# GpSimd taken out of the SSD mixer's groups: masks to ScalarE, products and sums to VectorE

## The chip, the cores and the metric

The kernel runs on one core of a Trainium2 chip. A core has five engines that run at the same time, each with its own instruction stream in a fixed order: TensorE (PE in the profile, PEld for its weight loads), VectorE (DVE), ScalarE (ACT), GpSimd (POOL), and SyncE (SP), which here issues DMA transfers. Instructions of different engines wait for each other through semaphores. The metric is the device time of one execution in microseconds (us).

## What is computed

Two transformer-like blocks of two layers each, on 256 latent tokens and 256 context tokens of width 1024. The first block's second layer holds the SSD mixer (a state space scan with 8 groups of 4 heads), which is where the change lies:

```python
def ssd_chunk_scan(xs, dt, a, bm, cm, s0):
    ...
    def step(s, inp):
        xi, dti, bi, ci = inp
        cum = jnp.cumsum(dti * a, axis=1)
        seg = cum[:, :, None] - cum[:, None, :]
        decay = jnp.exp(jnp.where(mask, seg, -jnp.inf))
        xdt = xi * dti[..., None]
        cb = jnp.einsum('bign,bjgn->bijg', ci, bi)
        y = jnp.einsum('bijg,bijgr,bjgrp->bigrp', cb, decay, xdt)
        y = y + jnp.einsum('bign,bigr,bgrpn->bigrp', ci, jnp.exp(cum), s)
        ...
def ssd_mixer(uc, ul, w_in, conv_w, conv_b, dt_bias, a_log, d_skip, norm_g, w_out, need_ctx):
    ...
        z, xbc, dt = jnp.split(h @ w_in, [SSD_DI, SSD_DI + SSD_CONV_DIM], axis=-1)
        xbc = jax.nn.silu(dwconv(xbc, conv_w, conv_b))
        ...
        y = (y_f + y_b[:, ::-1] + xs * d_gr).reshape(b, l, SSD_DI)
        return rms_norm(y * jax.nn.silu(z), norm_g) @ w_out, (s_f, s_b)
```

`y_f` and `y_b` are the scans forwards and backwards; both start from the states that the context tokens leave.

## The kernel before

All matrix products with weights go through `gemm`. It streams a weight in units of 128x1024 float32 (tile `wr`, three buffers), and `_unit` splits each into a high part `wh` (line 395, a cast on ScalarE) and a low part `wl` (line 400, a subtraction on the engine that `loeng` names at that time). There are two buffers each of `wh` and `wl`. The matmuls of line 439 then take high times high and low (`wh` with `xh` and `xl`), and low times high (`wl` with `xh`). So per unit the cast, then the subtraction, have to be done before TensorE comes to the unit.

The mixer's function `ssd` goes over 8 groups `g`. A group has four units of convolution channels (24 matmuls each, mostly of 512 columns), and two units for the gate `z` (24 matmuls of 256 columns each), whose `wl` is made on the engine that `SLO` names. The convolution is lines 1200 to 1210 (tiles `scv`, `sth`, `sxc`), then come transposes (L1244), scaled copies `sxs` and `sxk` (L1189) and the states (L1265, L1273). After that, for each of two token tiles `t`, this is done (shortened):

```python
                for d in range(2):
                    for i, x in enumerate((dah.bitcast(F32), dal)):
                        rt = self.t([P, 4, P], "srt", NRT, F32R)
                        ...
                        if RTE[i] == "s":
                            for r in range(4):
                                nc.scalar.mul(out=rt[:, r, :], in_=tri_in[:, d, :], mul=x[:, t, c + r:c + r + 1])
                        else:
                            eng = nc.vector if RTE[i] == "v" else nc.gpsimd
                            eng.tensor_tensor(out=rt, in0=tri_in[:, d, None, :].to_broadcast([P, 4, P]),
                                              in1=bc(x[:, t, c:c + 4], P), op=ALU.mult)
                        nc.tensor.matmul(out=p, lhsT=strict[:, d, :], rhs=rt.rearrange("p r c -> p (r c)"),
                                         start=d == 0 and i == 0, stop=d == 1 and i == 1)
```

These masks `srt` (two high, from `sdh`, and two low, from `sdl`; three buffers) feed four matmuls (L1302). Their exponential is `sL` (L1305). `sM` is made on ScalarE (L1310) and VectorE (L1315), then multiplied by `sL` (L1317, on the engine that `ME` names). L1327 multiplies it with the values. `syi` holds the part that comes from the state (L1322); two sums (L1331 and L1332, on GpSimd where `YP` is 1) and L1333 and L1334 finish the tile as `syg`, and L1340 transposes it.

The code is written group after group, but a scheduler sets the order of the instructions on each engine when the program is built, by its own estimates of how long each takes. So TensorE's stream has the next groups' weight products woven between one group's mixer steps, and other background work (`aps`, L533) too.

Of the kernel before, what the change touches and what calls it, by code (L numbers as in the profile page):

```python
# [29 lines left out]
EPRIO = 500  # L30
FSTOP = 7
SBEG = 0
SLO = "gpsimd"
MPOOL = (1,)
NRT = 3
RTE = "sg"
GPRIO = 300
GF = 150
GFIN = 26
# [21 lines left out]
BRAW = 1  # L61
NBSQ = 2
NBB = 2
VE, ME = "s", "g"
ENORM = ("vector", "vector")
NBTG, NBP, NQK, NBPT = 7, 3, 8, 2
SHQ, XB2 = 1, 18
XDA, XKA, XSA, RTA, YP = 0, 0, 0, 2, 1
GRATE = (0, 0.6, 0.6, 0.6)
GAINENG = "gpsimd"  # L70
CPRIO = 4000
# [199 lines left out]
class K:  # L271
# [889 lines left out]
    def ssd(self, u, mode):  # L1161
# [29 lines left out]
        for g in range(8):  # L1191
# [39 lines left out]
            def sink_z(p, t, sz=sz):  # L1231
                th = self.t([P, 2, 256], "sth", 2)
                nc.scalar.activation(out=th[:, 0], in_=p, func=AF.Tanh, scale=0.5)
                nc.vector.scalar_tensor_tensor(out=sz[:, t, :], in0=th[:, 0], scalar=1.0, in1=p, op0=ALU.add, op1=ALU.mult)
            jobs = [("T", 0, 256, 256 + t * P, P, (lambda p, t=t: sink_z(p, t))) for t in range(2)]
            with self.lo_on(SLO, True):
                off = self.gemm(A["swin"], off, KD, 256, u, jobs)
# [44 lines left out]
            for t in range(2):  # L1282
# [8 lines left out]
# [3 lines that stand above are left out]
                        c = d * 32 + g * 4  # L1294
# [6 lines that stand above are left out]
# [1011 lines left out]
```

## Time and profile before

| what | us |
|---|---|
| median of 3 runs (lowest to highest) | 2522.02 (2516.8 to 2524.46) |
| the profiled execution, and its span from first to last instruction | 2523.41, 2521.6 |
| busy in the span: TensorE | 2392.2 (95%) |
| VectorE | 1741.5 (69%) |
| ScalarE | 1208.9 (48%) |
| GpSimd | 363.6 (14%) |

The mixer's groups lie from about 880 to 1217 us of the span. A share of busy time is an average over stages with different limits. An engine's idle time costs something only where another engine waits for it in the end, so what counts for a stage is which engine has no idle time there, and whom it waits for when it has. The span of a matmul overlaps that of the next one, so the pace of TensorE is read from the distance between starts.

### The profile page before, as it was taken

The page shows a single profiled execution, that of the slowest core. Times are in us where ns is not written, and L with a number is a line of the kernel's source. Part 1 is how long each engine was busy: PE and PEld are TensorE (multiplying, and loading weights), DVE is VectorE, ACT ScalarE, POOL GpSimd, SP SyncE. Part 2 cuts the span into 40 slices and gives each one's busy share as a digit, 9 for nine tenths or more (in the row PEclk, how much of TensorE's full clock was granted, in tenths as well). Part 3 has the DMA queues.
Part 4 walks back from the last instruction along what each step waited for, and adds up shares of the span by engine and source line. Part 5 has one row for each costly group of instructions (what it writes and reads, how often), then busy time and mean ns, then how long its engine had stood idle before and what let it go on. Part 6 is the DMA issues. An engine that isn't in the chain of part 4 may idle for free.

```text
span 2521.6 us, 36806 instructions
## 1 busy us (share of the span) xinstructions
PE 2392.2 (95%) x13879; PEld 1913.8 (76%) x13879; DVE 1741.5 (69%) x3303; ACT 1208.9 (48%) x2367; POOL 363.6 (14%) x308
## 2 busy tenths in 40 slices
PE   7999997999998899999899989999999998999997
PEld 4777776777776777787698868788777877877776
DVE  3455578866688867687755676987564566798666
ACT  3445444432323455566565455554444344564553
POOL 0011114000000124443400120100021001100010
PEclk8999998999999899999999999999999999999999
DMA  6222244555555444523465552222122353333343
GB/s 253 100 85 76 86 166 151 192 200 213 201 198 177 158 159 143 175 84 113 162 216 184 191 164 90 77 72 84 59 84 76 106 191 118 125 107 100 109 147 130
DMA packets 105394, 348.01 MB, mean 138 GB/s; under 512 B 14200, under 2 KB 20288, under 8 KB 105216
## 3 DMA queue, kind: packets, MB, share of 16 engines
q1 hardware_dynamic: 100304, 333.22, 38.6%
q0 software_dynamic: 3616, 12.06, 1.4%
q8 instruction: 109, 1.79, 0.3%
q14 instruction: 69, 0.57, 0.1%
q10 hardware_dynamic: 1296, 0.38, 0.1%
HBM read 338.75 MB, written 6.85 MB: 137 GB/s over the span
## 4 chain that ended last, share of the span: by engine, by line
PE 45%; DVE 5%; ACT 1%; issue 1%; DMA 0%; DVEq 0%; ACTq 0%
PE acc L439 37%; PE ps L1728 2%; PE ps L1756 2%; PE aps L1867 1%; PE ps L1640 1%; DVE wl L400 1%; PE aps L1772 1%; PE acc L1640 0%; DVE xl L751 0%; PE ps L741 0%; DVE by L761 0%; DMA row<-rowd 0%; ACT wh L395 0%; DVE bnm L1739 0%; DVE bP L1853 0%
## 5 line engine op out<-in xcount | busy, mean ns | idle before, releaser
L395 ACT CAST wh<-wr 128x1024 fp32r<-128x1024 f32 (+3 forms) x461 | 471.9, 1026 | 637.1 <-PE acc L439 557.4
L439 PE MATMUL acc<-wh,xh 128*128 128x512 f32 (+3 forms) x1876 | 725.2, 393 | 11.9 <-ACT wh L395 6.5
L400 DVE TENSOR_TENSOR wl<-wr,wh 128x1024 fp32r<-128x1024 f32 (+3 forms) x421 | 517.3, 1230 | 314.2 <-ACT wh L395 238.7
L439 PE MATMUL acc<-wh,xl 128*128 128x512 f32 (+3 forms) x1876 | 718.6, 388 | 7.3 <-DVE xl L1570 7.0
L439 PE MATMUL acc<-wl,xh 128*128 128x512 f32 (+3 forms) x1876 | 507.1, 386 | 5.9 <-POOL wl L400 4.0
L439 PEld LDWEIGHTS acc<-wh,xh 128*128 128x128 f32 x1876 | 356.4, 191 | 96.0 <-ACT wh L395 12.2
L439 PEld LDWEIGHTS acc<-wh,xl 128*128 128x128 f32 x1876 | 356.9, 191 | 81.2 <-DVE xl L1570 8.3
L439 PEld LDWEIGHTS acc<-wl,xh 128*128 128x128 f32 x1876 | 342.8, 189 | 84.4 <-POOL wl L400 6.2
L439 PE MATMUL acc<-xl,wh 128*128 128x512 f32 (+2 forms) x1024 | 341.1, 349 | 9.6 <-DVE xl L751 9.5
L439 PE MATMUL acc<-xh,wh 128*128 128x512 f32 (+2 forms) x1024 | 345.6, 354 | 4.2 <-ACT wh L395 2.2
L439 PE MATMUL acc<-xh,wl 128*128 128x512 f32 (+1 forms) x1024 | 231.8, 347 | 4.3 <-DVE wl L400 4.3
L439 PEld LDWEIGHTS acc<-xh,wh 128*128 128x128 f32 (+1 forms) x1024 | 197.1, 194 | 39.0 <-issue 6.3
L439 PEld LDWEIGHTS acc<-xl,wh 128*128 128x128 f32 (+1 forms) x1024 | 197.8, 194 | 35.2 <-DVE xl L751 10.7
L400 POOL TENSOR_TENSOR wl<-wr,wh 128x1024 fp32r<-128x1024 f32 x40 | 98.3, 2461 | 724.5 <-ACT wh L395 583.5
L439 PEld LDWEIGHTS acc<-xh,wl 128*128 128x128 f32 x1024 | 166.5, 191 | 37.8 <-DVE wl L400 7.1
L573 DVE SCALAR_TENSOR_TENSOR adav<-wrd,s,adav 128x512 f32<-128x512 f32 x196 | 144.5, 769 | 55.4 <-DMA wrd<-in_ada 54.2
L1742 ACT ACTIVATE bP<-ps,bnm 128x512 f32<-128x512 f32 (+1 forms) x144 | 88.5, 621 | 86.2 <-DVE bnm L1739 70.8
L1988 POOL TENSOR_SCALAR bP<-bP,brc 128x512 f32<-128x512 f32 (+1 forms) x24 | 33.4, 1396 | 489.7 <-DVE brc L1985 461.2
L1739 DVE TENSOR_REDUCE bnm<-ps 128x1 f32<-128x512 f32 (+1 forms) x120 | 78.1, 683 | 32.3 <-PE ps L1728 32.0
L1204 DVE SCALAR_TENSOR_TENSOR scv<-acc,scw,scv 128x510 f32<-128x510 f32 (+3 forms) x140 | 83.4, 633 | 14.4 <-ACT scv L1200 14.2
L1756 PE MATMUL ps<-ident,bP 128*128 128x128 f32 x400 | 60.8, 278 | 2.4 <-ACT bPT L1631 1.4
L1631 ACT COPY bPT<-ps 128x512 f32<-128x512 f32 x75 | 43.8, 595 | 33.9 <-PE ps L1756 27.9
(429 smaller groups left out, 3097.8 us busy)
## 6 DMA issues: line engine op xcount, KB each, us to landing
wr<-in_w SPq DMA_DIRECT2D x136, 512.0 KB, 3.5
wr<-in_win SPq DMA_DIRECT2D x136, 512.0 KB, 3.5
wrd<-in_ada SPq DMA_DIRECT2D x128, 512.0 KB, 4.4
wr<-in_swin SPq DMA_DIRECT2D x52, 512.0 KB, 3.5
wr<-in_gwin SPq DMA_DIRECT2D x24, 512.0 KB, 3.4
wr<-in_wbr SPq DMA_DIRECT2D x24, 512.0 KB, 3.4
wr<-in_wout SPq DMA_DIRECT2D x24, 512.0 KB, 3.5
wst<-in_ada SPq DMA_DIRECT2D x16, 512.0 KB, 7.6
```

The costliest lines, as they stand in the source:

```text
L395: nc.scalar.copy(out=hi[:, :n], in_=raw[:, :n])
L400: getattr(nc, eng).tensor_tensor(out=lo[:, :n], in0=raw[:, :n], in1=hi[:, :n].bitcast(F32), op=ALU.subtract)
L439: mm = nc.tensor.matmul(out=o, lhsT=wv if kind == "F" else xv, rhs=xv if kind == "F" else wv, start=b["first"], stop=bool(fin and b["left" ...
L573: o = nc.vector.scalar_tensor_tensor(out=a, in0=xi, scalar=c, in1=a, op0=ALU.mult, op1=ALU.add)
L1204: nc.vector.scalar_tensor_tensor(out=c[:, :, o0:o1], in0=pv[:, :, i0:i1], scalar=w[:, tap:tap + 1], in1=c[:, :, o0:o1], op0=ALU.mult, op1= ...
L1631: return self.nc.scalar.copy(out=out, in_=in_)
L1640: nc.tensor.transpose(p[:width, t * P:(t + 1) * P], x[:, j * width:(j + 1) * width], self.ident)
L1728: mms.append(self.nc.tensor.matmul(out=p[:, n * nk:(n + 1) * nk], lhsT=q[a][rows, i * P:(i + 1) * P], rhs=k[b][rows, :nk], start=m == 0, s ...
L1739: nc.vector.tensor_reduce(out=nm[:, :n], in_=p.rearrange("p (n k) -> p n k", n=n), axis=AX.X, op=ALU.max, negate=True)
L1742: nc.scalar.activation(out=e[:, i * nk:(i + 1) * nk], in_=p[:, i * nk:(i + 1) * nk], func=AF.Exp, bias=nm[:, i:i + 1], accum_out=sm[i])
L1756: mms.append(nc.tensor.transpose(p[:, d:d + P], e[:, c:c + P], self.ident))
L1988: nc.gpsimd.tensor_scalar(out=b, in0=b, scalar1=rc[:, 1, i:i + 1], scalar2=None, op0=ALU.mult)
```

## The change

Four numbers change. No other line does.

```diff
-SLO = "gpsimd"
+SLO = "vector"
...
-RTE = "sg"
+RTE = "ss"
...
-VE, ME = "s", "g"
+VE, ME = "s", "v"
...
-XDA, XKA, XSA, RTA, YP = 0, 0, 0, 2, 1
+XDA, XKA, XSA, RTA, YP = 0, 0, 0, 2, 0
```

For each group: the two low parts of the gate's weights (L400) go from GpSimd to VectorE; the four low masks (one instruction of 128x512 each at line 1300) become 16 instructions of 128x128 on ScalarE (line 1297); the two products of line 1317 and the four sums of lines 1331 and 1332 go from GpSimd to VectorE. GpSimd keeps its work outside of the groups.

The scheduler also sets a new order. Besides the mixer's groups on all engines, it differs in one later piece, in the last attention layers of the second block (TensorE's rows 9933 to 10110 of 11001, at about 2260 to 2320 us), and SyncE issues ten of the loads of the mixer's weights at other places among its own.

On ScalarE, while the second group's token tiles are done: from the cast of the third group's first gate unit (the first `wh`) to that of its second (the other `wh`); `sdh` marks high masks, `sdl` low ones, and a row with x4 is one mask. Before:

```order
L395 CAST wh_8691<-wr_8689 128x1024
L1268 COPY sS_8385<-ps_8380 128x512
L1310 ACTIVATE sM_8420<-scb_8397,sdt_7611 128x128 x4
L1200 ACTIVATE scv_8647<-acc_8507,scw_7369 128x512
L1200 ACTIVATE scv_8657<-acc_8508,scw_7369 128x512
L1297 ACTIVATE srt_8451<-tri,sdh_7641 128x128 x4
L395 CAST wh_8737<-wr_8735 128x1024
L1305 ACTIVATE sL_8418<-ps_8399 128x512
```

Now:

```order
L395 CAST wh_8715<-wr_8713 128x1024
L1305 ACTIVATE sL_8436<-ps_8411 128x512
L1297 ACTIVATE srt_8481<-tri,sdh_7641 128x128 x4
L1200 ACTIVATE scv_8671<-acc_8531,scw_7369 128x512
L1200 ACTIVATE scv_8681<-acc_8532,scw_7369 128x512
L1297 ACTIVATE srt_8487<-tri,sdl_7642 128x128 x4
L1297 ACTIVATE srt_8859<-tri,sdh_7641 128x128 x4
L1297 ACTIVATE srt_8865<-tri,sdl_7642 128x128 x4
L1310 ACTIVATE sM_8495<-scb_8466,sdt_7611 128x128 x4
L395 CAST wh_8761<-wr_8759 128x1024
```

Between the two casts stood one mask; now there are four, of which the last two already belong to the third group's first token tile, and the products `sM` of the second token tile stand right ahead of the second cast.

On VectorE at the same place: from the third group's convolution taps (L1204) on its first two channel blocks, whose results lie in banks of `acc`, to the last step `sxc` of the convolution. Before:

```order
L1204 SCALAR_TENSOR_TENSOR scv_8647<-acc_8507,scw_7369,scv_8647 128x2x255
L1204 SCALAR_TENSOR_TENSOR scv_8657<-acc_8508,scw_7369,scv_8657 128x2x255
L1322 TENSOR_TENSOR syi_8433<-ps_8430,sex_7630 128x512
L1204 SCALAR_TENSOR_TENSOR scv_8647<-acc_8507,scw_7369,scv_8647 128x2x255
L1204 SCALAR_TENSOR_TENSOR scv_8657<-acc_8508,scw_7369,scv_8657 128x2x255
L1204 SCALAR_TENSOR_TENSOR scv_8647<-acc_8507,scw_7369,scv_8647 128x2x254
L1204 SCALAR_TENSOR_TENSOR scv_8657<-acc_8508,scw_7369,scv_8657 128x2x254
L1210 SCALAR_TENSOR_TENSOR sxc_8655<-sth_8653,scv_8647 128x512
L1210 SCALAR_TENSOR_TENSOR sxc_8665<-sth_8663,scv_8657 128x512
L1204 SCALAR_TENSOR_TENSOR scv_8667<-acc_8509,scw_7369,scv_8667 128x2x254
L1204 SCALAR_TENSOR_TENSOR scv_8677<-acc_8510,scw_7369,scv_8677 128x254
```

Now:

```order
L1334 TENSOR_TENSOR syg_8406<-syi_8451,ssz_8280 128x256
L1204 SCALAR_TENSOR_TENSOR scv_8671<-acc_8531,scw_7369,scv_8671 128x2x254
L1204 SCALAR_TENSOR_TENSOR scv_8681<-acc_8532,scw_7369,scv_8681 128x2x254
L1322 TENSOR_TENSOR syi_8508<-ps_8505,sex_7630 128x512
L1315 SCALAR_TENSOR_TENSOR sM_8495<-scb_8466,sdt_7611,sM_8495 128x128 x4
L1331 TENSOR_TENSOR syi_8508<-syi_8508 128x256
L400 TENSOR_TENSOR wl_8762<-wr_8759,wh_8761 128x1024
L1332 TENSOR_TENSOR syi_8508<-syi_8508,sxk_8390 128x256
L1317 TENSOR_TENSOR sM_8495<-sM_8495,sL_8493 128x512
L1210 SCALAR_TENSOR_TENSOR sxc_8679<-sth_8677,scv_8671 128x512
L1210 SCALAR_TENSOR_TENSOR sxc_8689<-sth_8687,scv_8681 128x512
L400 TENSOR_TENSOR wl_8985<-wr_8982,wh_8984 128x1024
```

The low part of the second gate unit (the first `wl`), both sums (L1331, L1332) and the product (L1317) have come between the taps and `sxc`; that low part stands behind the four `sM` instructions and one sum.

## Rows read from the trace of the kernel before

**Rows 1.** Windows: us, then busy us (instructions) PE, PEld, DVE, ACT, POOL; clock, DMA share, GB/s.

```profile
880.00:1200.00 320.00, 307.99 (x1760) 252.26 (x1760) 239.04 (x448) 186.30 (x432) 130.29 (x98) 0.99 0.39 134
2260.00:2320.00 60.00, 59.70 (x326) 47.70 (x325) 47.87 (x120) 31.01 (x56) 0.00 (x0) 1.00 0.33 105
```

**Rows 2.** Waits of PE, 880 to 1217 us: total us, times, longest us; nine lines.

```profile
PE ps L1265 <- DVE sxs L1189: 2.9, 2, 1.5
...
PE ps L1327 <- POOL sM L1317: 1.2, 1, 1.2
...
PE acc L439 <- ACT xh L473: 0.6, 1, 0.6
```

**Rows 3.** POOL's groups, 870 to 1225 us: busy us, mean ns; idle before, releaser.

```profile
L400 POOL TENSOR_TENSOR wl<-wr,wh 128x1024 fp32r<-128x1024 f32 x17 | 40.4, 2381 | 83.8 <-PE acc L439 51.2 <-ACT wh L395 24.6 <-issue 8.0
...
L1300 POOL TENSOR_TENSOR srt<-tri,sdl 128x512 fp32r<-128x512 f32 x32 | 39.2, 1245 | 77.0 <-PE ps L1302 66.1 <-DVE sdl L1224 10.9
...
L1317 POOL TENSOR_TENSOR sM<-sM,sL 128x512 f32<-128x512 f32 x16 | 24.7, 1541 | 25.7 <-ACT sL L1305 12.5 <-DVE sM L1315 7.1 <-ACT srt L1297 4.1
...
L1332 POOL TENSOR_TENSOR syi<-syi,sxk 128x256 f32<-128x256 f32 x16 | 15.9, 996 | 0.9
...
L1331 POOL TENSOR_TENSOR syi<-syi 128x256 f32<-128x256 f32 x16 | 13.3, 831 | 20.4 <-DVE syi L1322 20.4
```

**Rows 4.** Three of DVE's groups in the same stretch, all of two operands in SBUF.

```profile
L400 DVE TENSOR_TENSOR wl<-wr,wh 128x1024 fp32r<-128x1024 f32 x44 | 59.4, 1354 | 22.2 <-ACT wh L395 21.6 <-PE acc L439 0.4
...
L1210 DVE SCALAR_TENSOR_TENSOR sxc<-sth,scv 128x512 f32<-128x512 f32 x21 | 21.2, 1014 | 0.6 <-ACT sth L1207 0.5
...
L1334 DVE TENSOR_TENSOR syg<-syi,ssz 128x256 f32<-128x256 f32 x16 | 11.5, 716 | 0.2
```

**Rows 5.** Timeline of DVE, 1069 to 1078 us: start us, us.

```profile
1074.39 2.44 DVE L1210 SCALAR_TENSOR_TENSOR sxc<-sth,scv 128x512 f32<-128x512 f32 x1
```

**Rows 6.** Timeline of POOL, the same stretch.

```profile
1073.87 2.41 POOL L400 TENSOR_TENSOR wl<-wr,wh 128x1024 fp32r<-128x1024 f32 x1
```

**Rows 7.** Three lines of code on DVE, whole span: ns least/median/most, first and last start.

```profile
L1210 DVE SCALAR_TENSOR_TENSOR sxc<-sth,scv x35: 407/679/2442, 856.3 to 1163.7; 128x512 f32<-128x512 f32 x21, 128x256 f32<-128x256 f32 x14
...
L1334 DVE TENSOR_TENSOR syg<-syi,ssz x16: 407/426/1523, 916.1 to 1212.6; 128x256 f32<-128x256 f32 x16
...
L400 DVE TENSOR_TENSOR wl<-wr,wh x421: 548/1225/3383, 36.4 to 2511.0; 128x1024 fp32r<-128x1024 f32 x131, 128x384 fp32r<-128x384 f32 x4, 128x768 fp32r<-128x768 f32 x3, 128x576 fp32r<-128x576 f32 x2
```

**Rows 8.** ACT's group of the high masks, 870 to 1225 us.

```profile
L1297 ACT ACTIVATE srt<-tri,sdh 128x128 fp32r<-128x128 f32 x128 | 41.0, 391 | 16.9 <-PE ps L1302 15.0 <-DVE sdh L1223 1.9
```

**Rows 9.** Timeline of PE, 948 to 958 us, with a wait at a gate unit.

```profile
949.66 0.39 PE L439 MATMUL acc<-xl,wh 128*128 128x512 f32 x1
949.89 0.40 PE L439 MATMUL acc<-xh,wh 128*128 128x512 f32 x1
...
950.48 0.59 PE L1320 MATMUL ps<-sS,sxc 128*128 128x256 f32 x2
950.91 0.59 PE L1320 MATMUL ps<-sT,sxc 128*128 128x256 f32 x2
...
951.46 0.28 PE L439 MATMUL acc<-xh,wh 128*128 128x256 f32 x1
951.58 0.28 PE L439 MATMUL acc<-xl,wh 128*128 128x256 f32 x1
...
954.72 0.36 PE L439 MATMUL acc<-wh,xh 128*128 128x256 f32 x1 [1.92 <-ACT srt L1297]
```

**Rows 10.** Timeline of ACT, the same stretch: the cast that PE waited for.

```profile
951.94 1.05 ACT L395 CAST wh<-wr 128x1024 fp32r<-128x1024 f32 x1 [0.87 <-ACT srt L1297]
```

**Rows 11.** Timeline of DVE, the same stretch: taps in turn on two banks.

```profile
952.52 2.71 DVE L1204 SCALAR_TENSOR_TENSOR scv<-acc,scw,scv 128x510 f32<-128x510 f32 x4
```

**Rows 12.** Timeline of PE, 962 to 967 us: a background product.

```profile
962.35 1.06 PE L533 MATMUL aps<-wrd,s 128*32 128x512 f32 x8
```

**Rows 13.** Timeline of DVE, 962 to 967 us: four instructions of line 1315.

```profile
965.43 1.13 DVE L1315 SCALAR_TENSOR_TENSOR sM<-scb,sdt,sM 128x128 f32<-128x128 f32 x4
```

## Prediction

> **What bounds the kernel now.** Begin with the windows view of the mixer's stretch [rows 1]. Between 880 and 1200 us TensorE is busy for 308.0 of 320 us, VectorE for 239.0 (75%), ScalarE for 186.3 (58%) and GpSimd for 130.3 (41%), and TensorE's granted clock is 0.99. So TensorE bounds the stage, and it can win at most its idle time: 12.0 us, 0.5% of the whole. Next look at whom it waits for in these 12 us: nine lines of the view of waits, from 2.9 down to 0.6 us [rows 2]. GpSimd ends only one of them, 1.2 us, where the product `sM` (L1317) is late for L1327. GpSimd's groups [rows 3] show why it ends so little: its masks sat for 66.1 us waiting for TensorE to free a buffer, and its low parts for 51.2 us waiting for TensorE to finish with an earlier unit. It is mostly ahead of its consumer.
>
> So the change is not read from shares. It is read from whether ScalarE and VectorE, whose streams now hold that work as well, are still ahead of TensorE at the places where TensorE takes it.
>
> **What is removed.** GpSimd loses 39.2 us of masks, 24.7 of products, 13.3 and 15.9 of sums, and 16 of its 17 low parts at 2.38 us, 38.1 [rows 3]: 131.2 us. None of that is itself on the path, except the 1.2 us.
>
> **What VectorE gets.** 16 low parts at 1.225 us are 19.6. For the 16 products of 128x512, an operation that the trace has only on GpSimd, the nearest row is another one of VectorE with two operands in SBUF and 512 columns: median 0.679, so 10.9 us. For the 32 sums of 128x256 it is L1334, median 0.426, so 13.6 [rows 7]. Together 44.1 us. The other end for a product is GpSimd's own 1.54 [rows 3], which would make it 57.8; I take the first, since it is the same engine and the same size.
>
> **What VectorE gets back.** The same three lines take longer on average in this stage than their medians [rows 4, 7]: `wl` 1.354 against 1.225, 44 times, 5.7 us; `sxc` 1.014 against 0.679, 21 times, 7.0; L1334 0.716 against 0.426, 16 times, 4.6. That is 17.3 us. A pair of rows shows where it goes: a `sxc` that begins 0.5 us after a low part on GpSimd takes 2.44 us [rows 5, 6]. That is 1.76 more than its median, and nearly the rest of GpSimd's instruction (1073.87 + 2.41 = 1076.28). Without GpSimd this falls away. VectorE's load is then 239.0 + 44.1 - 17.3 = 265.8 of 320 us, 83%.
>
> The page "SBUF — State Buffer" of the Trainium skill, section "Who interferes with whom", says why: a VectorE instruction with two inputs in SBUF and a GpSimd instruction that reads SBUF want the same port, and the one that comes second is blocked until the first is through. Rows 5 and 6 agree. By that rule everything that VectorE does late in this stage could be GpSimd's doing, which is the second rival below; by the rows it is 17.3 us of busy time, which is a gain only where TensorE was waiting.
>
> **What ScalarE gets.** 32 low masks of four instructions. The high ones are 128 instructions in 41.0 us [rows 8], so 0.32 each and 1.28 a mask; the low ones cost another 41.0. Load: 186.3 + 41.0 = 227.3 of 320 us, 71%. The path from a free buffer to a mask gets longer: GpSimd's mask took 1.25 [rows 3] beside ScalarE's, and now they come one behind the other.
>
> A rule of the skill speaks against this part: "ScalarE: Activation LUTs", section "Rules for kernel authors", sends plain products to VectorE and budgets about 0.3 us for each instruction and 0.83 ns for each element. By that a mask of four would be an estimated 1.62 us and the sum 10.9 us more ScalarE time. The rows, at 0.32 an instruction in a run of four, are what I use.
>
> **Is the work still in time?** I follow one place by hand, that of the order shown above. Count from the start of the second tile's first L1302, which frees a mask buffer. TensorE's way to the second gate unit: two more L1302 and 0.23 to the start of the next, at 0.235 each, 0.70; background products 1.06 [rows 12]; five products of the convolution, two of 512 and three of 256 columns, 0.82; L1320 0.86; the fourth L1302 0.235; the first gate unit, 24 at 0.118, 2.83. Sum 6.5 us (the distances between starts are 0.235, 0.43 for a pair of L1320, and 0.118 [rows 9]). ScalarE's way to that unit's cast: some 0.5 us until the buffer is free (an estimate: about one matmul's 0.4 us [rows 9] and a little), three masks 3.84, four `sM` taken at the same 1.28, the cast 1.05 [rows 10]: 6.7. So the high part is late by 0.2. The low part: VectorE has `sM` from ScalarE at 5.6, needs 1.13 for its own four [rows 13], 0.4 for one sum and 1.225: about 8.4, and TensorE wants it 8 matmuls (0.94) after 6.5, at 7.4. Late by 1.0, of which the high part's delay is a share. In four of the eight groups three masks, or nearly so, stand ahead of a gate unit's cast; in the later groups they stand behind it. The four are not all as tight, so I count 0.9 in each: **+3.6 us**.
>
> The other place is the accumulator. A gate unit needs a bank of `acc`, and the taps of the first channel block have to let go of it. At 954.72 TensorE stood for 1.92 us ahead of a gate unit [rows 9]. The row names ScalarE's mask, but the cast had been done at 952.99 [rows 10]; the taps on VectorE, in turn on two banks, ended between 954.5 and 955.2 [rows 11], so I take the bank to be what was missing. In the new order a low part and a product (1.225 + 0.679 = 1.9) have come between the first and the last tap of that block in two groups; in the others there is a sum, or nothing new. I count half of it in two groups: **+1.9 us**.
>
> GpSimd's own wait goes: **-1.2 us**. The other 9 us or so that VectorE and ScalarE end I leave as they are: VectorE has 27 us more in its queue and no surprises in it.
>
> The moved loads of SyncE cost nothing as long as the 16 DMA engines are at 0.39 [rows 1]. The new order at 2260 to 2320 us can win no more than TensorE's 0.3 us of idle time there; VectorE is at 80% and GpSimd idle, so I count nothing.
>
> **Sum:** 3.6 + 1.9 - 1.2 = +4.3 us on the profiled execution's 2523.41: 2527.7. That execution lies 1.4 us above the median of the runs, 2522.02, so the forecast is **2526 us**. A difference under 0.3%, 7.6 us, can't be told from none; the forecast is no measurable change, slightly on the slow side.
>
> **Rivals.**
> *ScalarE becomes the engine that TensorE waits for.* The low and high masks are made one behind the other, so each of the 16 token tiles can be late by one mask, 1.28 us: 20.5 us, 2542. For it: at the one place followed by hand ScalarE is late already; its queue holds masks of the next group ahead of a cast. Against it: 71% load, buffers filled ahead, and only half of the groups in that order. It decides once the lateness at a tile exceeds about 0.5 us in all eight groups. Chance 0.25.
> *The release of VectorE wins.* All waits that VectorE and GpSimd end go, some 10 of the 12 us; 2522 - 10 = 2512. For it: the lock of rows 5 and 6, and work that is half as long on VectorE. Against it: VectorE has more to do on balance, and half of its waits are of a kind (taps, `sxs`) that no GpSimd instruction stands in front of. Chance 0.16.
> *VectorE's burst between groups.* The two low parts (2.45 us) fall into the taps, `sxc` and `sxs` of seven group changes, where PE waits for `sxs` most [rows 2]: 7 x 2.45 = 17, 2539. Chance 0.09.
>
> **Chances and range.** Forecast 0.50, its own range 2517 to 2532. The first and third rivals are slower by over 0.3%, and so is a tail of the forecast (2529.6 lies within its range): 0.36. Faster by over 0.3%, below 2514.5: most of the second rival, 0.14. No measurable change: 0.50. The range for 8 in 10 goes from 2513, short of the whole release, to 2541, about the price of the mask on every tile.
>
> **What would show it.** Right, if TensorE's busy time over the mixer's 320 us stays within some 5 us of 308, GpSimd has next to nothing there, `sxc` and L1334 come at 0.68 and 0.43, the added ScalarE group is 41 us and the low parts of the gate 1.23 each. The waits of TensorE should name casts and low parts at gate units. Wrong, if waits for masks (`srt`) or casts add up to over 10 us, if the clock in the stage falls below 0.97, or if waits for `sxs`, `xl` and taps have gone. A difference that arises after 1240 us would speak against all of it.

## The result, and the profile after

The changed kernel takes 2541.27 us (median of 4 runs, 2536.89 to 2545.65), the kernel before 2520.51 (4 runs): a ratio of 1.0088, 95% interval 1.0069 to 1.0107. It is slower by about 21 us, where no measurable change was forecast.

All of it arises in the mixer's groups. The first product with the masks (L1302) starts at 900.0 us before and 901.4 after, the last at 1207.1 and 1230.4: the stage has grown by 21.9 us. The span has grown by 19.7 (2521.6 to 2541.3). So nothing is added behind the groups.

The windows view of the changed kernel, with the columns of [rows 1]: the mixer's 320 us, then single slices of 10 us.

```profile
880.00:1200.00 320.00, 295.39 (x1655) 241.71 (x1648) 241.04 (x477) 204.75 (x520) 12.08 (x8) 0.96 0.37 124
...
1000.00:1010.00 10.00, 7.70 (x31) 5.70 (x32) 6.34 (x18) 3.61 (x12) 0.00 (x0) 0.60 0.31 112
...
1140.00:1150.00 10.00, 6.03 (x19) 4.50 (x18) 9.05 (x21) 6.89 (x22) 0.00 (x0) 0.76 0.24 83
1150.00:1160.00 10.00, 10.00 (x54) 8.61 (x53) 3.67 (x6) 3.30 (x7) 0.00 (x0) 0.90 0.08 14
```

Against [rows 1], TensorE is idle for 24.6 us instead of 12.0, which is 12.6 more, and its granted clock is 0.96 instead of 0.99, which is 0.03 x 320 or about 10 us more (the clock is rounded, and 0.01 of it is 3 us here). Together that is about the 21.9. VectorE and ScalarE did not come to their limit over the stage (241 and 205 of 320 us). The low clock is not spread out: it stands in a few slices, each with a long wait in it or just ahead of it.

The waits of TensorE in the changed kernel, 880 to 1240 us (total us, times, longest us), which answer to [rows 2]:

```profile
PE acc L439 <- DVE scv L1204: 14.1, 7, 4.0
PE aps L533 <- DMA wrd<-in_ada: 8.8, 4, 3.9
PE acc L439 <- ACT wh L395: 1.5, 1, 1.5
PE acc L439 <- DVE wl L400: 1.2, 2, 0.9
PE ps L1302 <- ACT srt L1297: 0.9, 1, 0.9
```

The same view of the kernel before has the first of them at:

```profile
PE acc L439 <- DVE scv L1204: 1.9, 2, 0.9
```

Two waits carry the loss. The first is for a bank of `acc` that the convolution's taps still read: 14.1 us where there were 1.9. The second is for a refill of `wrd`, the weights of the background products: 8.8 us, not in the list of before at all. Waits for casts, low parts and masks, where the prediction looked, are small.

What the change does to durations came as forecast. Two lines of code of the changed kernel, whole span (least/median/most ns), and ScalarE's two groups of masks, 870 to 1250 us (these answer to [rows 7, 8]):

```profile
L1210 DVE SCALAR_TENSOR_TENSOR sxc<-sth,scv x35: 417/685/693, 855.8 to 1193.3; 128x512 f32<-128x512 f32 x21, 128x256 f32<-128x256 f32 x14
...
L1334 DVE TENSOR_TENSOR syg<-syi,ssz x16: 414/420/426, 915.4 to 1235.5; 128x256 f32<-128x256 f32 x16
```

```profile
L1297 ACT ACTIVATE srt<-tri,sdh 128x128 fp32r<-128x128 f32 x128 | 41.1, 395 | 1.6 <-DVE sdh L1223 1.6
L1297 ACT ACTIVATE srt<-tri,sdl 128x128 fp32r<-128x128 f32 x128 | 40.9, 393 | 12.4 <-PE ps L1302 12.4
```

The long `sxc` (2.44 us) and L1334 (1.52 us) of [rows 7] are gone: the most is now 0.693 and 0.426. That is the blocking between VectorE and GpSimd that the prediction read from [rows 5, 6], and it falls away with GpSimd's work. The Trainium skill ("SBUF — State Buffer", section "Who interferes with whom") states this blocking, and these numbers agree with it.

**One wait followed by hand.** The longest wait for a bank ends at 1146.00. TensorE's timeline of the changed kernel around it (start us, us; in brackets the idle time ahead and what ended it):

```profile
1123.98 0.86 PE L439 MATMUL acc<-xh,wl 128*128 128x512 f32 x4
...
1139.38 0.40 PE L439 MATMUL acc<-xh,wh 128*128 128x512 f32 x1
1139.61 0.39 PE L439 MATMUL acc<-xl,wh 128*128 128x512 f32 x1
...
1141.40 0.63 PE L439 MATMUL acc<-xh,wl 128*128 128x512 f32 x2
1146.00 0.80 PE L439 MATMUL acc<-xh,wh 128*128 128x512 f32 x1 [3.97 <-DVE scv L1204]
...
1147.02 0.63 PE L439 MATMUL acc<-xh,wh 128*128 128x512 f32 x1
1147.45 0.63 PE L439 MATMUL acc<-xl,wh 128*128 128x512 f32 x1
```

The seventh group's channel products end by 1124.84 (first row), so its banks are full then; the masks at that time are the sixth group's. A group has four blocks of channels. Each is read from its bank by one instruction on ScalarE (L1200), then by four taps on VectorE (L1204); then come a tanh on ScalarE (L1207) and a product on VectorE (L1210), which lets go of the buffer `scv`. There are two such buffers, so the third block's L1200 has to wait for the first block's L1210. ScalarE's timeline of the changed kernel, from there on:

```profile
1122.30 1.45 ACT L1200 ACTIVATE scv<-acc,scw 128x512 f32<-128x512 f32 x2
1124.22 1.05 ACT L395 CAST wh<-wr 128x1024 fp32r<-128x1024 f32 x1 [0.47 <-ACT scv L1200]
1126.61 0.59 ACT L1268 COPY sS<-ps 128x512 f32<-128x512 f32 x1 [1.34 <-PE ps L1265]
1127.92 1.28 ACT L1297 ACTIVATE srt<-tri,sdl 128x128 fp32r<-128x128 f32 x4 [0.73 <-PE ps L1302]
1129.11 1.27 ACT L1297 ACTIVATE srt<-tri,sdh 128x128 fp32r<-128x128 f32 x4
1130.28 1.27 ACT L1297 ACTIVATE srt<-tri,sdl 128x128 fp32r<-128x128 f32 x4
1131.45 0.58 ACT L1305 ACTIVATE sL<-ps 128x512 f32<-128x512 f32 x1
1131.93 1.28 ACT L1310 ACTIVATE sM<-scb,sdt 128x128 f32<-128x128 f32 x4
1133.10 1.28 ACT L1297 ACTIVATE srt<-tri,sdh 128x128 fp32r<-128x128 f32 x4
1134.27 1.15 ACT L1207 ACTIVATE sth<-scv 128x512 f32<-128x512 f32 x2
...
1136.26 0.78 ACT L1200 ACTIVATE scv<-acc,scw 128x512 f32<-128x512 f32 x1
```

The first two blocks are read at 1122.30. The third one's L1200 comes at 1136.26, 11.4 us after the channel products were done, behind two low masks, two high ones, `sL`, `sM` and the tanh of the first two blocks. Then VectorE takes over. Its timeline in the changed kernel, from the third block's first tap to the pair that begins with its last (0.74 us, so until 1145.94):

```profile
1137.95 0.74 DVE L1204 SCALAR_TENSOR_TENSOR scv<-acc,scw,scv 128x508 f32<-128x508 f32 x1
...
1139.27 1.21 DVE L400 TENSOR_TENSOR wl<-wr,wh 128x1024 fp32r<-128x1024 f32 x1
...
1145.20 1.13 DVE L1204 SCALAR_TENSOR_TENSOR scv<-acc,scw,scv 128x508 f32<-128x508 f32 x2
```

Among the taps stand a low part, sums, parts of `sM`, `syi` and `scb`. VectorE is without a gap from 1133.6 to past 1146, and TensorE waits for the bank until 1146.00. In the kernel before, the same two steps of the same group were:

```profile
1106.26 1.45 ACT L1200 ACTIVATE scv<-acc,scw 128x512 f32<-128x512 f32 x2 [0.92 <-PE acc L439]
...
1115.04 0.78 ACT L1200 ACTIVATE scv<-acc,scw 128x512 f32<-128x512 f32 x1 [0.21 <-DVE sxc L1210]
```

There the tanh and the third block came ahead of all masks, 8.8 us behind the first two blocks instead of 14.0. The bracket of the second row names the turn of the buffers: ScalarE waited for `sxc` (L1210).

**The wait for `wrd`.** TensorE and SyncE's queue in the changed kernel at the longest of these waits:

```profile
996.16 1.06 PE L533 MATMUL aps<-wrd,s 128*32 128x512 f32 x6
...
1002.30 1.93 PE L533 MATMUL aps<-wrd,s 128*32 128x512 f32 x8 [3.95 <-DMA wrd<-in_ada]
```

```profile
997.24 0.80 SPq L525 DMA_DIRECT2D wrd<-in_ada  x2
```

There are two `wrd` buffers. The refill is issued when the earlier products have read them (997.24), and in TensorE's new order the next background products come so close behind that they wait for the transfer until 1002.30, 5 us after the issue.

### The profile page after: what moved, and what is told of

Read it like the earlier page. It is cut to its first block, busy times and chain, and to the rows that moved or that the text cites. A ratio compares the mean times of both kernels' runs of the same rounds, so it can differ in the third digit from the quotient of the medians.

```text
span 2541.3 us, 36848 instructions
## 1 busy us (share of the span) xinstructions
PE 2398.7 (94%) x13879; PEld 1919.5 (76%) x13879; DVE 1755.3 (69%) x3367; ACT 1245.9 (49%) x2495; POOL 236.8 (9%) x212
## 4 chain that ended last, share of the span: by engine, by line
PE 45%; DVE 4%; ACT 1%; issue 1%; DMA 1%; POOL 0%; SPq 0%; DVEq 0%; ACTq 0%; POOLq 0%
PE acc L439 37%; PE ps L1728 2%; PE ps L1756 1%; PE aps L1867 1%; PE ps L1640 1%; PE aps L1772 1%; DVE wl L400 1%; DVE xl L751 0%; ACT wh L395 0%; PE acc L1640 0%; POOL wl L400 0%; DMA bsq<-in_gr 0%; PE ps L741 0%; DVE bnm L1739 0%; DVE xl L1718 0%
## 5 line engine op out<-in xcount | busy, mean ns | idle before, releaser
L400 DVE TENSOR_TENSOR wl<-wr,wh 128x1024 fp32r<-128x1024 f32 (+3 forms) x437 | 535.4, 1227 | 309.1 <-ACT wh L395 234.2
L400 POOL TENSOR_TENSOR wl<-wr,wh 128x1024 fp32r<-128x1024 f32 x24 | 60.3, 2518 | 761.4 <-ACT wh L395 704.9
L1204 DVE SCALAR_TENSOR_TENSOR scv<-acc,scw,scv 128x254 f32<-128x254 f32 (+3 forms) x140 | 84.5, 636 | 10.9 <-ACT scv L1200 10.7
```

What stands on the lines that cost most here:

```text
L400: getattr(nc, eng).tensor_tensor(out=lo[:, :n], in0=raw[:, :n], in1=hi[:, :n].bitcast(F32), op=ALU.subtract)
L1204: nc.vector.scalar_tensor_tensor(out=c[:, :, o0:o1], in0=pv[:, :, i0:i1], scalar=w[:, tap:tap + 1], in1=c[:, :, o0:o1], op0=ALU.mult, op1= ...
```

## The experiments

The theory at the end: what costs is time on ScalarE or VectorE between the filling of an `acc` bank and its release, and so the third block's late start. Its rivals: the added work costs at its own consumers; the refills of `wrd` are the larger part; the scheduler's new order is at fault by mere luck. The letters in the expectations are each run's own and are explained there.

**The four parts alone** (each is one line of the change; the other three lines stay as before).

```
SLO = "vector"        # e1      RTE = "ss"         # e2
VE, ME = "s", "v"     # e3      YP = 0             # e4
```

> The change's first part alone: the low parts of the gate's weights on VectorE. Theory A (VectorE's stream became too long between the convolution's taps, so that banks of acc are released late; the waits of TensorE for scv of 14.1 us and the clock that falls after them): 16 subtractions of 1.22 us stand among the taps, so this part alone gives a third to a half of the 20 us, 2526 to 2532. Theory B (ScalarE with the low masks is what is late): this part alone gives nothing, 2518 to 2523.

> The second part alone: the low masks on ScalarE. Theory A: 41 us more on ScalarE, nothing on VectorE, waits for scv stay near the 1.9 us of before; 2518 to 2525. Theory B: most of the 20 us is here, 2532 to 2541. In both, GpSimd still blocks VectorE, less often.

> The third part alone: 16 products of 128x512 on VectorE instead of GpSimd, 0.68 us each. Theory A: 10.9 us of work for VectorE, a quarter of what it got, so some 2 to 6 us: 2522 to 2527. Theory B: nothing, 2518 to 2523, or a few us faster, since GpSimd's late product (1.2 us of waits) goes.

> The fourth part alone: 32 sums of 128x256 on VectorE instead of GpSimd, 0.42 us each. Theory A: 13.6 us of work for VectorE, some 2 to 6 us: 2522 to 2527. Theory B: nothing, 2518 to 2523.

Measured: gate low parts on VectorE 2522.76 us (1.0027, 1.0013 to 1.0041), low masks on ScalarE 2534.58 (1.0071, 1.0053 to 1.0089), products 2527.05 (1.0037, 1.0023 to 1.0051), sums 2517.32 (1.0001, 0.999 to 1.0011), against 2518.05 for the kernel before. So the low masks cost most, 17 us alone; the products 9, the low parts 5, the sums nothing. The parts sum to 29.5 us (16.5 + 9.0 + 4.7 - 0.7) where the whole change costs 21: they are not additive. Theory B's ranges hold e1 and e2; e3 lies at the upper edge of Theory A's, and e4 just below Theory B's. The parts on VectorE do not cost by the wait for the bank: `scv` is not in e3's list of waits at all and has 0.6 us in e1's (where `sM` leads with 7.2), so their 9 and 5 us are not explained here. The masks alone bring both waits of the changed kernel. Its waits of TensorE, 880 to 1235 us:

```profile
PE acc L439 <- DVE scv L1204: 8.8, 5, 2.3
PE aps L533 <- DMA wrd<-in_ada: 6.8, 4, 3.7
PE ps L1327 <- POOL sM L1317: 5.1, 4, 1.7
```

**The change without its masks, and with cheaper ones.** In e5 the low masks go back to GpSimd. In e6 each low mask is one instruction of 128x512 that scales all four heads by the first head's factor, so the other three heads' own scaling is left out.

```
-RTE = "ss"
+RTE = "sg"                       # e5
```
```
-for r in range(4):
+if i == 1:                       # e6
+    nc.scalar.mul(out=rt, in_=tri_in[:, d, None, :].to_broadcast([P, 4, P]), mul=x[:, t, c:c + 1])
+for r in range(4 if i == 0 else 0):
```

> The change with the low masks back on GpSimd; gate, products and sums stay on VectorE. Theory B (the masks on ScalarE cost most, as their 17.9 us alone suggest): most of the 20 us comes back, 2519 to 2526. Theory A (VectorE's 44 us of new work cost most, in whatever company): 2530 to 2538. The parts measured alone (6.8 for the gate, 9.3 for the products, 0 for the sums) would add up to 2534.

> The changed kernel with each low mask made by one ScalarE instruction of 128x512 instead of four of 128x128; all four heads of a group then take the first head's scale, so the scaling of the other three is left out. If ScalarE's time in the masks is what costs (41 us, now about 19): half of the masks' part comes back, 2528 to 2534. If it is only where the scheduler puts them and what it moves, the time stays within 3 us of the changed kernel's, 2536 to 2542.

Measured: e5 2525.71 us (1.0017, 0.9997 to 1.0037), e6 2526.53 (1.0017, 1.0002 to 1.0032), the kernel before 2520.93. Taking the masks away returns 15.6 us of the changed kernel's 2541.27, making them shorter returns 14.7, more than either reading of e6 had forecast. A mask in e6 took 0.715 us (median) instead of 1.28: 32 x 0.565 = 18 us less ScalarE time, spread over a stage that ScalarE does not fill. So it is ScalarE's time at certain places that costs, though both edits also move the order, and what each of the two is worth is not separated. The waits for `scv` are 3.6 us in e5 and 8.8 in e6; the latter is as much as in e2, which takes 8 us longer.

**Shorter taps, in both kernels.** Two of the convolution's four taps on VectorE are left out.

```
-for tap in (0, 1, 3, 4):
+for tap in (1, 3):               # e7 on the changed kernel, e8 on the kernel before
```

> The changed kernel with two of the convolution's four taps on VectorE left out (so half of the time between the end of a product and the release of its bank of acc). To be read against the next kernel. If the late release by VectorE is the path of the loss, the waits for scv (14.1 us) and the clock that falls after them go, and it comes within 6 us of the kernel before with the same taps left out. If ScalarE's masks or the background loads are the path, 12 us or more remain between the two.

> The kernel before with the same two taps left out, as the measure for the last one. TensorE had 12 us to win in the stage, of which 3.8 hung on the taps: 2510 to 2520 by both theories.

Measured: e7 2527.19 us (1.0021, 1.0006 to 1.0036), e8 2530.07 (1.0034, 1.0018 to 1.005). The difference between the kernels is gone and e7 waits 3.6 us for `scv`, as the late release by the taps would have it, but the control was a miss: with less work the kernel before became 9 us slower, with waits of 10.8 us for `sM` and 4.3 for `syg`. The scheduler had made another order, and I put the 9 us down to it, though no run shows the order by itself. So this pair weighs little.

**Background products and banks.** First the background products are kept out of the groups (e9, e10), except that 48 of 96 still come at the end of the last ones, from 1172.8 us on in e9 and 1149.8 in e10. Then the bank that they leave free is given to the gates' columns, so that the four banks of `acc` serve four channel blocks and have a whole group to be released in (e11, e12).

```
-SRATE = 1
+SRATE = 0                                                                    # e9 to e12
-                off = self.gemm(A["swin"], off, KD, 256, u, jobs)
+                off = self.gemm(A["swin"], off, KD, 256, u, jobs, ("aps", 1))  # e11, e12
```

> The changed kernel with no background products of the modulation weights inside the mixer's groups; they follow behind the groups, so the whole time says little and the stage is read: the first and last product with the masks (L1302) and the waits of TensorE between. In the changed kernel those lie 329 us apart, of which 14.7 are background products, 8.8 waits for `wrd` and about 5 the clock behind them. Theory A (the refills of `wrd` are the larger part of the loss): about 300 us, and at most 10 more than the kernel before with the same edit. Theory B (the accumulators' late release by the taps is the larger part): about 305 to 312 us, 12 or more above the kernel before with the same edit, with the waits for `scv` still over 10 us.

> The kernel before with the same edit, the control: 307 us between the first and the last product with the masks, less the 13.8 of background products, about 293 us, by both theories.

> The changed kernel without background products in the groups, and with the bank that they leave free used as the accumulator of the gates' columns, so that each of the other four banks has a whole group to be released in. Theory B: the waits for `scv` fall below 3 us and the stage comes within 5 us of the kernel before with the same two edits. Theory C (the order of the instructions costs, whichever wait shows it): other waits take their place, and the stage stays 12 us or more above it.

> The kernel before with the same two edits, the control: 288 to 293 us, since its waits for `acc` are few (the control without the fifth bank is to give about 293).

Measured: e9 2601.74 us (1.0326, 1.0296 to 1.0356), e10 2574.37 (1.0218, 1.0186 to 1.025), e11 2575.00 (1.0216, 1.0186 to 1.0245), e12 2580.16 (1.0241, 1.0207 to 1.0275). All four are slower than both kernels, as the background work comes later; what counts is each pair. With the background products moved away the changed kernel is 27 us behind its control, so they are not the larger part of the loss. From first to last L1302 it takes 319.0 us and the control 299.8; both lengths are above those expected, and the 19 us between them are what the late release by the taps was to leave (12 or more). With a bank more it is 5 us ahead of its control, and its stage is 2 us longer than the control's (309.8 and 307.4 us; 288 to 293 was expected for the control). The same wait in e9 and in e11, 880 to 1235 us:

```profile
PE acc L439 <- DVE scv L1204: 21.6, 10, 4.0
```

```profile
PE acc L439 <- DVE scv L1204: 0.3, 1, 0.3
```

These lengths say less than the waits, since more background products have come into the stage (56 in e11 and 64 in e12, against 48).

**The same with the background products in place.** The gates' accumulator is taken from the three banks of the small products.

```
+                off = self.gemm(A["swin"], off, KD, 256, u, jobs, ("ps", 3))   # e13 changed, e14 before
```

> The changed kernel with its background products where they were, and the accumulator of the gates' columns taken from the three banks of the small products, so that the four banks of `acc` again serve one group each. Theory B (late release by the taps): waits for `scv` under 4 us, and the time within 8 us of the control with the same edit. Theory C (any order of the changed kernel costs): 15 us or more above the control, by other waits.

> The control, the kernel before with the same edit: it has little wait for `acc` to lose and one bank of three less for the small products for part of each group, so 2520 to 2535 us.

Measured: e13 2582.61 us (1.0249, 1.0232 to 1.0267), e14 2594.94 (1.0302, 1.0282 to 1.0321). The control was missed by 60 us: with two banks left for the small products for part of each group, waits for `sM` came to 33.8 us in e13 and 29.0 in e14. As a remedy it is useless. As a test it agrees: the waits for `scv` are gone from the list, and the changed kernel is not slower than its control but 12 us faster.

**Another order, nothing else.** The background products are asked for at 0.8 instead of 1 a unit.

```
-SRATE = 1
+SRATE = 0.8                      # e15 on the changed kernel, e16 on the kernel before
```

> The changed kernel with the background products asked for at 0.8 instead of 1 a unit, which only spreads them: the same instructions in another order. Theory B: the waits for `scv` remain (10 us or more) and those for `wrd` shrink below 5, so 2530 to 2538. Theory C (the loss is the luck of one order): it may come anywhere from 2520 to 2550.

> The control for the luck of an order: the kernel before with the same spreading. Theory B: 2517 to 2525, as nothing in it waits long. Theory C: up to 10 us above that, as when two taps were left out of it.

Measured: e15 2552.99 us (1.0128, 1.0101 to 1.0155), e16 2519.18 (1.0002, 0.999 to 1.0014). The kernel before doesn't notice; the changed one gets 12 us worse, above both ranges. So the loss is not the luck of one order, as far as one other order can tell. But its name changes with the order: in e15 the waits are 9.4 us for `sM`, 9.1 for `wrd`, 6.1 for `scv`. The expectation of 10 us or more for `scv` and under 5 for `wrd` was wrong.

**The masks on VectorE.**

```
-RTE = "ss"
+RTE = "sv"                       # e17, on the changed kernel
```

> The change with its low masks on VectorE instead of ScalarE, so that GpSimd still has no part in the groups: 32 products of 128x512, at 0.68 us as VectorE's other products of that size (L1317) about 22 us on VectorE where ScalarE had 41. If ScalarE's time ahead of the convolution is what holds the banks: 2522 to 2530. If the two engines that release a bank are one chain and work on either holds it (the taps themselves are VectorE's): 2535 to 2550, with waits for `scv` or `sM` over 10 us.

Measured: 2532.89 us (1.006, 1.0037 to 1.0082), between the two ranges; the 32 masks took 0.680 us each as expected, and the waits of TensorE, 880 to 1240 us, begin with:

```profile
PE acc L439 <- DVE scv L1204: 12.3, 6, 5.0
```

It is 8 us better than with the masks on ScalarE, though the intervals of the two still overlap (1.0069 to 1.0107 there). The Trainium skill ("ScalarE: Activation LUTs", section "Rules for kernel authors") sends a plain product to VectorE; the durations here agree, 0.680 us of VectorE against 1.28 of ScalarE. But the wait for the bank is still there. Time on either engine of the chain holds it.

**One more buffer.** The changed kernel with three buffers of `scv`, so that the third block no longer needs the first one's product. No work is added or removed.

```
-                c = self.t([P, 2, 256], "scv", 2)[:, :ns]
+                c = self.t([P, 2, 256], "scv", 3)[:, :ns]   # e18, on the changed kernel
```

> The changed kernel with three instead of two buffers of `scv`, so that the first step of a third channel block (L1200) no longer waits until the first block's tanh (L1207) and product (L1210) are through behind ScalarE's masks. If this chain is what holds the banks of `acc`: waits for `scv` under 5 us in the groups and 2520 to 2531 us. If the banks are held by VectorE's load alone: no change from the changed kernel, 2536 to 2546.

Measured: 2522.55 us (12 runs; 1.0009, 0.9997 to 1.0021, against 2519.89 in 17 runs). The whole loss is gone but for a rest that can't be told from none. ScalarE's timeline of e18 at the same place (the sixth group's first L1302 is at 1117.35):

```profile
1112.23 1.45 ACT L1200 ACTIVATE scv<-acc,scw 128x512 f32<-128x512 f32 x2
...
1115.11 0.77 ACT L1200 ACTIVATE scv<-acc,scw 128x512 f32<-128x512 f32 x1
...
1117.86 1.28 ACT L1297 ACTIVATE srt<-tri,sdl 128x128 fp32r<-128x128 f32 x4 [0.73 <-PE ps L1302]
```

The third block follows the first two after 2.9 us, ahead of the masks, though the same masks stand in ScalarE's stream as in the changed kernel. Of its waits (880 to 1240 us), the longest first, and its window these rows answer to the changed kernel's:

```profile
PE ps L1327 <- DVE sM L1317: 5.8, 4, 2.5
...
PE ps L1302 <- ACT srt L1297: 3.7, 4, 1.0
...
PE aps L533 <- DMA wrd<-in_ada: 0.9, 2, 0.7
...
PE acc L439 <- DVE scv L1204: 0.4, 1, 0.4
```

```profile
880.00:1200.00 320.00, 306.92 (x1742) 251.50 (x1739) 250.06 (x496) 212.89 (x541) 11.18 (x8) 0.99 0.38 131
```

TensorE is busy for 306.9 us again and the clock is back at 0.99. Even the waits for `wrd` are down to 0.9 us, with no change to its buffers. Waits for `sM` and for masks have grown in their place, from 0.8 and 0.9 us to 5.8 and 3.7. The buffer also brought a new order, so a part of the 19 us may be the order's; e18 by itself can't tell, but both of the signs that were set for it before it ran, time and wait, came true.

**Twelve kernels on one scale.** These are the ones with all four taps, the banks as they were and the background products in the groups. The distance from the first block's L1200 to the third one's, read from ScalarE's timeline and averaged over seven groups, beside the time (the runs were made on several chips, where the kernel before took 2518.1 to 2520.9):

| kernel | distance, us | time, us |
|---|---|---|
| before | 9.4 | 2520.5 |
| sums alone (e4) | 10.3 | 2517.3 |
| before at 0.8 (e16) | 10.3 | 2519.2 |
| products alone (e3) | 10.5 | 2527.1 |
| change without masks (e5) | 10.9 | 2525.7 |
| low parts alone (e1) | 11.5 | 2522.8 |
| masks on VectorE (e17) | 11.9 | 2532.9 |
| masks of one instruction (e6) | 12.3 | 2526.5 |
| masks alone (e2) | 13.1 | 2534.6 |
| the change | 14.3 | 2541.3 |
| the change at 0.8 (e15) | 14.3 | 2553.0 |
| the change, three buffers (e18) | 4.1 | 2522.6 |

The two columns go together, with a scatter of up to 7 us (and 12 in e15) that the distance does not explain. By itself the table shows a connection only; that the distance is a cause rests on e18, which changes the buffers behind it and nothing else but the order that follows from them.

## Why the prediction was wrong

**What bounds the kernel** was right: TensorE, with VectorE and ScalarE below their limits. That TensorE's busy time would stay within 5 us of 308 was wrong (295.4).

**What is removed, and what VectorE gets back**, was right in size: the maxima of `sxc` and L1334 fell to their medians. It was rightly not counted as a gain, and it wasn't one.

**What ScalarE gets**: 41.0 us forecast, 40.9 measured; each instruction at 0.32, as taken.

**The first term, +3.6 us** for late casts and low parts at gate units, did not come. Waits for `wh` and `wl` add up to 2.7 us (1.5 + 1.2, where `wl` had 1.1 before), but none of them is at a gate unit: those for `wl` are at channel products (927.83 and 929.96), the one for `wh` is at 1222.17 in the product that TensorE takes up after the last gate. That the size comes near is luck.

**GpSimd's own wait, -1.2 us**, went, but `sM` from VectorE has 0.8 us in its place. The other waits, some 9 us that were left as they were, have shrunk to 3.9: all waits of the changed kernel but those for `scv`, `wrd` and `sM`.

**The second term, +1.9 us, is the step that failed.** The kind of wait was the right one: "The other place is the accumulator", where the taps let go of a bank. Its price was not, nor were most of its places. The prediction looked at gate units, where 3.7 of the 14.1 us are (the longest at 1049.18). Another 7.0 are at the next group's channel products (the longest is the one followed by hand, at 1146.00), and 3.4 at the product after the last gate:

```profile
1049.18 0.35 PE L439 MATMUL acc<-wh,xh 128*128 128x256 f32 x1 [2.25 <-DVE scv L1204]
...
1105.11 0.50 PE L439 MATMUL acc<-xh,wh 128*128 128x512 f32 x1 [2.69 <-DVE scv L1204]
...
1189.24 0.50 PE L439 MATMUL acc<-wh,xh 128*128 128x512 f32 x1 [3.36 <-DVE scv L1204]
```

I counted what comes between the first and the last tap on VectorE (1.9 us, half of it, in two groups). I did not follow the chain back to where the taps come from: L1200 on ScalarE, and behind it the turn of the two `scv` buffers through a tanh on ScalarE and a product on VectorE. That chain passes ScalarE's queue twice for every third block, and the new masks stand in that queue, in every group. It measured 12.2 us more waiting (14.1 against 1.9). In e18, where a third buffer cuts the chain, the wait is 0.4 us and 19 of the 21 us are back.

**Costed at nothing, and not nothing:** the background loads. The prediction's sentence on loads, "The moved loads of SyncE cost nothing as long as the 16 DMA engines are at 0.39", is about the mixer's weights and looks at the engines' load, which is still 0.37. The loads of `wrd`, which did cost, are not in it, nor how close their consumers stand in TensorE's order behind a ring of two buffers: 8.8 us. These waits come and go with the order (0.9 us in e18), so they follow from it and are no price of a load.

**Not in the sum at all:** the clock. About 10 us of the 21.9 are TensorE running at the lower level behind its waits. The prediction had a clock under 0.97 as a sign of being wrong, and no term for it.

**The rivals.** ScalarE as the engine that TensorE waits for gave 2542, next to the result, but by another mechanism: each tile late by one mask, so waits for `srt`, which measured 0.9 us. The masks on ScalarE were the larger part, and they acted on the convolution in the same queue and not on their own consumers. The release of VectorE did not win: GpSimd's waits went, and new ones came. For the burst between groups the waits for `sxs` should have grown; they left the list.

**What stays open.** Why the scheduler put the masks ahead of the first tanh is not shown; it works with its own estimates. In its new order the sixth group's first L1302 also comes sooner after the seventh group's first two L1200 (5.1 us, from 1122.30 to 1127.41, instead of 10.9), so how much of the delay is the masks' length and how much the order is not separated. How the loss splits between waits for the bank and the order's other waits is open too: e15 has the same distance, less waiting for `scv` and 12 us more time. The 9 and 5 us of e3 and e1 came without this wait. And three buffers were not tried on the kernel before, so whether it would gain from them is not known.

## What to carry to other kernels

When work moves onto an engine that isn't full, don't ask first who consumes that work: ask which chains pass this engine's queue more than once, and what they hold meanwhile (here a bank of the accumulator and one of two buffers). Follow a buffer's release back over every engine to the start of the chain, not only the last instruction before it. Where a ring of two ties the third user to the first through two engines, one more buffer can be worth more than any placement: here the kernel with it was 19 us faster, of 21 lost.

## What the runs showed of the hardware

**A wait costs more than its length.** Behind the 3.97 us of waiting that end at 1146.00, products of 512 columns start 0.43 us apart (1147.02, 1147.45) instead of 0.23 (1139.38, 1139.61): the lower of TensorE's two clock levels, 1.2 instead of 2.4 GHz. The slices 1140 to 1150 and 1150 to 1160 have a granted clock of 0.76 and 0.90, so 0.24 x 10 + 0.10 x 10, some 3.4 us at full clock, are lost there, nearly all of it behind the wait. At 1000 to 1010 it is 0.60, where the 3.95 us wait for `wrd` ends. The length of a wait does not settle it: 2.25 us of waiting that end at 1049.18 were followed by 0.84 in the slice 1050 to 1060, while 2.69 us at 1105.11 left that slice and the next at 1.00, and so did, in the kernel before, 1.92 us at 954.72 [rows 9].

**Four short instructions against a long one on ScalarE.** A mask of four instructions of 128x128 takes 1.28 us, one of 128x512 0.715 (e6): the same 512 columns, in little more than half the time.
